# LayerNorm's mean from two float32r products, and nine operations of a depthwise convolution moved from VectorE to ScalarE and to transfers that add

## The chip, the cores and the metric

One core of a Trainium2 chip runs the whole layer. The metric is the device time of one execution in microseconds, the median of several runs. The five engines run their own instruction streams and meet through semaphores: TensorE (PE in the profile; its weight loads stand apart as PEld), VectorE (DVE), ScalarE (ACT), GpSimd (POOL) and SyncE (SP). SP issues the loads from HBM; POOL issues the transfers that add what they carry to what lies at their destination ("adding transfers" below).

## The reference, cut to what matters

A block of a streaming encoder over 512 positions and 1024 channels, in float32: a feed-forward half step, then a mixer that has a convolution branch and a gated linear attention branch beside each other, an output projection over both, a second feed-forward half step, and a gated input embedding. The change touches the convolution branch.

```python
h = h + 0.5 * _swiglu(_rmsnorm(h, ffn1_norm), ffn1_w_in, ffn1_w_out)
z = _rmsnorm(h, mix_norm) @ w_in
conv_a, conv_gt, q, k, v, r, g_lr = jnp.split(z, SPLIT_POINTS, axis=-1)
y_conv = _conv_module(conv_a, conv_gt, conv_w, conv_b, conv_ln_g, conv_ln_b)
y_gla = _gla(q, k, v, r, g_lr, gate_w_up, gate_b, gla_norm)
h = h + jnp.concatenate([y_conv, y_gla], axis=-1) @ w_out
...
def _conv_module(a, b, w_dw, b_dw, ln_g, ln_b):
    glu = a * jax.nn.sigmoid(b)                      # 512 channels
    y = causal depthwise convolution of glu, 31 taps per channel, + b_dw
    return jax.nn.silu(_layernorm(y, ln_g, ln_b))    # mean and variance over the 512 channels
```

## The kernel before, in words

Everything is held transposed, channels on the 128 partitions and the 512 positions along a row, so 512 channels are four blocks of 128x512. Products are exact to about float32: each operand is cut into a high part (a float32r copy, made by ScalarE, `high`) and a low part (what is left, made by a subtraction on VectorE, `low`, or by ScalarE and an adding transfer of POOL, `added`), and a product is the sum of high times high, high times low and low times high, each a float32r matmul.

The mixer is written out by hand in the order in which its work shall run. With `in_order(True)` each of TensorE, VectorE and ScalarE executes its own calls in the order of the code; POOL's and SP's calls are placed by the scheduler of the tile framework. The parts that matter here come in this order:

- The four blocks of `glu` are made one after the other (`glu_gate`, `glu_value`, `glu_out`). Each starts a generator, `conv_steps(c)`: one step that begins the accumulator `acc[c]` with the last tap and the bias (a TENSOR_SCALAR on VectorE), and 30 steps that each add one tap (a SCALAR_TENSOR_TENSOR on VectorE, in place on `acc[c]`). Nothing waits for them for long, so they are VectorE's filling: `taps(n)` runs n steps at some place of the code, in turn from the two oldest blocks that are not finished, so that neighbouring steps mostly belong to different accumulators. A call of `next` that finds a block finished counts as one of the n.
- q, k and v are projected; `tokblock(wv, t)` makes v for four blocks of 128 positions, t = 0 to 3. The attention scores follow (`scores`, where POOL clears the tiles `sc` first), then r (`tokblock(wr, t)`) with the attention outputs in between (`outputs`).
- The outputs' row norms: VectorE forms `ms`, POOL raises it to the power -1/2 (the row `rs<-ms,negh 128x16`), VectorE refines that to `rso`, ScalarE scales the outputs by it into four tiles `ytok`, VectorE multiplies each by `rt`, and TensorE transposes them (`ps<-ident,r` for the first, `ps<-ident,y` for the other three). At the same place POOL issues adding transfers for some weights that are wanted later (`px`, `sm`, `wa`; `early_parts`, `ohigh`).
- ScalarE and VectorE make the attention half of the mixer's result (`yg`, `gsplit`), and TensorE multiplies it with the output weights, block after block (`first_part(n, ...)`, twelve matmuls each).
- What is left of the convolution's taps runs then (`for steps in list(conv)`), the four accumulators are summed into `acc012`, and the mean over 512 channels is a product of a constant matrix of 1/512 with that sum, in the midst of `first_part(5, ...)`:

```python
mub = aux()
first_part(5, wo[5], {6: lambda: pe.matmul(mub, mean, acc012, start=True, stop=True)})
```

Both operands are float32 here. The variance, the normalisation and the second half of the output projection follow.

In the profile, tiles from one shared set of buffers (`bt`) carry the name of the pair they lie in: the sum `acc012` stands as `r`, the third block of `glu` as `glu` or `glu_3512`, the fourth as `en`; `cv` are the accumulators (3195 the third block's, 3196 the fourth's). All calls of an engine go through one recording line, L46, so rows are told apart by their tiles.

Of the kernel before, what the change touches and what calls it, by code (L numbers as in the profile page):

```python
# [8 lines left out]
F32 = mybir.dt.float32  # L9
F32R = mybir.dt.float32r  # L10
I32 = mybir.dt.int32
AF = mybir.ActivationFunctionType
ALU = mybir.AluOpType
PSUM = bass.MemoryType.PSUM

P = 128
SEQ = 512
# [3 lines left out]
D_CONV = 512  # L21
WIDTH = 31
PAD = WIDTH - 1
# [39 lines left out]
def block_kernel(ctx: ExitStack, tc: tile.TileContext, a: dict, out: bass.AP):  # L63
    nc = tc.nc
    pe, dve, act, pool = (Ordered(tc, e) for e in (nc.tensor, nc.vector, nc.scalar, nc.gpsimd))
# [6 lines left out]
    cp = ctx.enter_context(tc.tile_pool(name="const", bufs=1))  # L72
# [23 lines left out]
    def bt(dt=F32, s="a"):  # L96
        if dt not in other:
            t, other[dt] = bt2(dt, s)
            return t
        return other.pop(dt)  # L100
# [4 lines left out]
    def tmp(s, w=SEQ, dt=F32, bufs=2):  # L105
        return tp.tile([P, w], dt, tag=s, bufs=bufs, name=nm(s))
# [65 lines left out]
    cw = col[:, ncol - DC:]  # L172
# [5 lines left out]
    def vec(name, c, n=1):  # L178
        at = first_of[name] + c
        return col0[:, at:at + n] if at < DC else col[:, at - DC:at - DC + n]  # L180
# [8 lines left out]
    def split(src, s, alloc=bt):  # L189
        hi, lo = bt2(s=s) if alloc is bt else (alloc(F32R, s + "H"), alloc(F32R, s + "L"))  # L190
        h_, l_ = hi, lo
        if len(src.shape) == 3:
            h_, l_ = (t.rearrange("p (k c) -> p k c", k=src.shape[1]) for t in (hi, lo))
        act.copy(h_, src)
        dve.tensor_tensor(out=l_, in0=src, in1=h_.bitcast(F32), op=ALU.subtract)
        return hi, lo
# [26 lines left out]
    def high(r3):  # L223

        nk, nc_ = r3.shape[1], r3.shape[2]
        hi = wp.tile([P, 1024], F32R, tag="wh", bufs=6, name=nm("wh"))
        lo = wp.tile([P, 1024], F32R, tag="wl", bufs=6, name=nm("wl"))
        h3 = hi[:, :nk * nc_].rearrange("p (k c) -> p k c", k=nk)
        l3 = lo[:, :nk * nc_].rearrange("p (k c) -> p k c", k=nk)
        act.copy(h3, r3)  # L230
        return h3, l3, r3

    def low(w, engine=dve):
        h3, l3, r3 = w
        engine.tensor_tensor(out=l3, in0=r3, in1=h3.bitcast(F32), op=ALU.subtract)
        return h3, l3

    def added(w):

        h3, l3, r3 = w  # L240
        act.mul(l3, r3, -1.0)
        pool.dma_start(out=l3.bitcast(F32), in_=r3, accum_op=ALU.add)
        return w
# [29 lines left out]
    def zblock(w, x, mid={}):  # L273

        ps = bank()
        for k in range(DC):
            if k in mid:
                mid[k]()
            wh, wl = rows_of(w, k)
            mm3(ps, wh, wl, *x[k], k == 0, k == DC - 1)  # L280
        return ps
# [305 lines left out]
    made = []  # L587

    def constants():
        mean = cp.tile([P, P], F32, name="mean")  # L590
        pool.memset(mean, 1.0 / D_CONV)
        m1, m2 = (bt(s="m1")[:, 0:4 * CH].rearrange("p (c t) -> p c t", t=CH) for _ in range(2))
        mask = cp.tile([P, 4, CH], I32, name="mask")
        pool.memset(m1, 1.0)
        pool.memset(m2, 1.0)
        pool.affine_select(out=m1, in_=m1, compare_op=ALU.is_gt, fill=0.0, base=0,
                           pattern=[[0, 4], [-1, CH]], channel_multiplier=1)
        pool.affine_select(out=m2, in_=m2, compare_op=ALU.is_gt, fill=0.0, base=-CH,
                           pattern=[[0, 4], [-1, CH]], channel_multiplier=1)
        pool.tensor_copy(mask[0:CH], m1[0:CH])  # L600
        pool.tensor_copy(mask[CH:P], m2[CH:P])
        nbias = cp.tile([P, 2], F32, name="nbias")
        for j in range(2):
            dve.tensor_scalar(nbias[:, j:j + 1], vec("gate_b", j), -1.0, None, ALU.mult)
        made[:] = mean, mask, nbias
# [404 lines left out]

    glu, acc, conv = [], [cvt() for _ in range(4)], []

    def conv_steps(c):
        y, g, tap = acc[c], glu[c], cw[:, c * WIDTH:(c + 1) * WIDTH]
        dve.tensor_scalar(y, g, tap[:, PAD:WIDTH], vec("conv_b", c), ALU.mult, ALU.add)
        yield
        for w in range(PAD):
            late = PAD - w
            dve.scalar_tensor_tensor(out=y[:, late:], in0=g[:, 0:SEQ - late], scalar=tap[:, w:w + 1],
                                     in1=y[:, late:], op0=ALU.mult, op1=ALU.add)  # L1020
            yield
# [3 lines left out]
    def taps(n):  # L1025

        for _ in range(n):
            if not conv:
                return
            i = turn[0] % min(2, len(conv))  # L1030
            turn[0] += 1
            try:
                next(conv[i])
            except StopIteration:
                conv.pop(i)
# [8 lines left out]
    def glu_value(ps):  # L1044
        a1 = tmp("u1")
        dve.tensor_tensor(out=a1, in0=ps, in1=rsb, op=ALU.mult)
        return a1

    def glu_out(a1, sg):
        g = bt(s="glu")  # L1050
        dve.tensor_tensor(out=g, in0=a1, in1=sg, op=ALU.mult)
        glu.append(g)
        conv.append(conv_steps(len(glu) - 1))
# [77 lines left out]
    cums, epos, eneg, edec, decay, ends = [], [], [], [], [], []  # L1131
    taps(10)
    glu_out(glu_value(pa), sg)
    pb = zblock(w2b[1], hg)
    taps(5)
    for j in range(2):
# [92 lines left out]
    def scores(j, between):  # L1229
        p4s = [bank().rearrange("p (u c t) -> p u c t", u=2, t=CH) for _ in range(2)]  # L1230
        ss = []
        for i in range(2):
            s = bt(s="sc").rearrange("p (c t) -> p c t", t=P)
            pool.memset(s, 0.0)
            ss.append(s)
        for u, (kk, qq) in enumerate(((kneg[j], qdec[j]), (kpos[j], qneg[j]))):
            for c in range(0, NCH, 2):
                for i in range(2):
                    d = slice(i * HK, (i + 1) * HK)
                    for cc in (c, c + 1):  # L1240
                        s0 = (cc % 2) * CH
                        cs = slice(cc * CH, (cc + 1) * CH)
                        pe.matmul(p4s[i][s0:s0 + CH, u, c // 2, :], kk[d, cs], qq[d, cs], start=True, stop=True)
        hs = [slice(i * CH, (i + 1) * CH) for i in range(2)]
        for s, p4 in zip(ss, p4s):
            for h in hs:
                act.copy(s[h, :, h], p4[h, 0])
        between()
        for s, p4 in zip(ss, p4s):
            for h in hs:  # L1250
                dve.copy_predicated(s[h, :, h], mask[h], p4[h, 1])
        sc.extend(ss)
# [60 lines left out]
    for t in range(TB):  # L1313
        ps = tokblock(wv, t, {8: lambda: wr.append(high(raw_r[2])),
                             14: lambda: wr.append(high(raw_r[3]))} if t == 3 else {})
        if t == 0:
            wr += [added(high(raw_r[i])) for i in range(2)]
            k_out(1, k1)
            taps(3)
        elif t == 1:  # L1320
            taps(4)
        elif t == 2:
            taps(3)
        else:
            taps(5)
            low(wr[2])
            taps(2)
            low(wr[3])
        v = bt(s="v")
        act.activation(v, ps, AF.Copy, scale=rs2[:, t:t + 1])  # L1330
        vt.append(v)
        if t == 1:
            for j in range(2):
                scores(j, lambda: taps((6, 4)[j]))
            for j in range(2):
                kp = bank()
                for i in range(TB):
                    pe.transpose(kp[:, i * P:(i + 1) * P], kdec[j][:, i * P:(i + 1) * P], ident)
                kd = bt(s="kdt")
                act.copy(kd, kp)  # L1340
                kdt.append(kd)
# [40 lines left out]
    def first_part(n, w, mid={}):  # L1382
        ps = bank()
        part(ps, w, range(4, 8), True, False, mid)
        half[n] = (w, ps)
# [72 lines left out]
            pass  # L1458
    conv.clear()
    dve.tensor_tensor(out=acc012, in0=acc012, in1=acc[3], op=ALU.add)  # L1460
    low(wo[3])
    ffn2_in = a["ffn2_w_in"]
    wf = {i: Left(ffn2_in, 2 * i) for i in range(3)}
# [2 lines left out]
    w1.fetch("a11", "a12")  # L1466
    first_part(4, wo[4])
    mub = aux()
    first_part(5, wo[5], {6: lambda: pe.matmul(mub, mean, acc012, start=True, stop=True)})
    first_part(2, wo[2])  # L1470
    sqs, lln, yc = [], [], []
    for c in range(4):
# [339 lines left out]
        dve.scalar_tensor_tensor(out=q, in0=r, scalar=nh, in1=r, op0=ALU.mult, op1=ALU.mult)  # L1812
        dve.scalar_tensor_tensor(out=q, in0=q, scalar=1.5, in1=r, op0=ALU.add, op1=ALU.mult)

    def scaled_out(t, e, src, *queue):
        y = bt(s="y")
        act.activation(y, src, AF.Copy, scale=roots[t][2])
        put(t, e, y, *queue)

    def put(t, e, y, queue=nc.sync):  # L1820
        queue.dma_start(out=out[0, t * P:(t + 1) * P, e * SEQ:(e + 1) * SEQ], in_=y)

    def first_half(t, e):
        y = bt(s="y")
# [117 lines left out]
    first_half(0, 0)  # L1942
    scaled_out(0, 1, gained)
    newton(1)
    scaled_out(1, 0, hf[1], act)
    second_half(1, 1)


# [48 lines left out]
```

## Time and profile before

| | |
|---|---|
| median of 3 runs | 921.92 us (921.84 to 922.2) |
| the profiled execution | 921.48 us, of which the span from first to last instruction is 919.7 us |
| granted TensorE clock | 0.998 |
| busy: PE, PEld, DVE, ACT, POOL | 99%, 85%, 89%, 56%, 7% of the span |
| bytes moved by transfers | 118.89 MB, mean 129 GB/s |
| PE busy from 454 to 484 us | 15.90 of 15.90 us to 470, 4.92 of 5.00 us to 475, 8.70 of 9.00 us to 484 |
| DVE busy from 370 to 484 us | all of it but 2.5 us |

Rows of the timeline give the start in microseconds from the span's start, the time taken, the engine, the operation, output <- inputs, how many such instructions the row merges, and in brackets how long the engine sat idle before it and what released it. A matmul's time runs from its start to the end of its pipeline, so rows of PE overlap; what one costs is the distance from start to start. The convolution stands from 361 us (the first block's first step) to 483 us (the last sum).

### The profile page before, as it was taken

How to read it: one execution, taken by the hardware profiler on the slowest of the kernel's cores; microseconds unless marked ns; L12 is line 12 of the kernel's file. 1: busy time of each engine (PE TensorE's matmuls, PEld its weight loads, DVE VectorE, ACT ScalarE, POOL GpSimd, SP SyncE). 2: the span in 40 equal slices, each digit the busy share in tenths (PEclk: the TensorE clock that was granted, in tenths of full speed). 3: DMA queues.
4: the chain of work that ended last, by engine and by line, in shares of the span. 5: the costliest groups of instructions: out<-in, count | busy, mean ns of one | idle time of the engine just before them, and what ended most of it. 6: DMA issues, size and time to landing. Idle time of an engine off the chain costs nothing.

```text
span 919.7 us, 12838 instructions
## 1 busy us (share of the span) xinstructions
PE 910.7 (99%) x4948; PEld 779.7 (85%) x4948; DVE 816.7 (89%) x1090; ACT 511.7 (56%) x746; POOL 60.3 (7%) x76
## 2 busy tenths in 40 slices
PE   9999999999999999999999999999999999999996
PEld 8899888888888887788887889888888888888885
DVE  6699989999989766999996779899999999997896
ACT  7755354445454574463665875455445444556884
POOL 0120000000000111001130020000000000000121
PEclk9999999999999999999999999999999999999999
DMA  9534333224334692245572563333223322358454
GB/s 350 186 100 136 117 112 122 91 73 135 115 92 115 158 295 51 69 118 158 139 166 93 137 157 97 115 116 126 87 84 130 122 89 87 118 155 240 92 99 131
DMA packets 37149, 118.89 MB, mean 129 GB/s; under 512 B 4192, under 2 KB 4960, under 8 KB 37088
## 3 DMA queue, kind: packets, MB, share of 16 engines
q1 hardware_dynamic: 30176, 97.22, 31.8%
q0 software_dynamic: 6624, 20.58, 12.5%
q8 instruction: 39, 0.64, 0.3%
q10 hardware_dynamic: 288, 0.27, 0.1%
q14 instruction: 22, 0.18, 0.1%
HBM read 96.43 MB, written 2.10 MB: 107 GB/s over the span
## 4 chain that ended last, share of the span: by engine, by line
PE 96%; DVE 2%; ACT 1%; issue 0%; POOLq 0%
PE ps L46 56%; PE pd L46 40%; DVE cv L46 1%; ACT wa L46 0%; ACT sq L46 0%; DVE yg L46 0%; DVE r L46 0%; DVE y L46 0%; ACT r L46 0%; ACT sm L46 0%; ACT px L46 0%; POOLq L1993 0%; ACT s L46 0%; DVE u L46 0%; DVE g L46 0%
## 5 line engine op out<-in xcount | busy, mean ns | idle before, releaser
L46 DVE TENSOR_TENSOR wl<-wr,wh 128x1024 fp32r<-128x1024 f32 (+2 forms) x159 | 185.9, 1179 | 16.9 <-ACT wh L46 16.4
L46 ACT CAST wh<-wr 128x1024 fp32r<-128x1024 f32 (+2 forms) x177 | 175.4, 1023 | 14.4 <-PE ps L46 7.7
L46 PE MATMUL pd<-hg,wh 128*128 128x512 f32 x576 | 150.0, 391 | 0.0
L46 PE MATMUL ps<-act,wh 128*128 128x512 f32 x448 | 137.9, 389 | 0.0
L46 PEld LDWEIGHTS pd<-hg,wh 128*128 128x128 f32 x576 | 105.9, 188 | 21.1 <-DVE u L46 0.4
L46 PE MATMUL ps<-hg,wh 128*128 128x512 f32 (+1 forms) x448 | 117.0, 345 | 0.0
L46 PEld LDWEIGHTS ps<-act,wh 128*128 128x128 f32 x448 | 84.1, 188 | 17.5
L46 ACT ACTIVATE s<-g 128x512 f32<-128x512 f32 x48 | 30.4, 632 | 117.6 <-DVE g L46 117.6
L46 PE MATMUL pd<-t,wh 128*128 128x512 f32 x392 | 95.3, 391 | 0.0
L46 ACT COPY sq<-pd 128x1024 f32<-128x1024 f32 x45 | 45.8, 1017 | 86.7 <-PE pd L46 52.3
L46 PE MATMUL ps<-act,wl 128*128 128x512 f32 x224 | 87.1, 389 | 0.0
L46 PEld LDWEIGHTS ps<-hg,wh 128*128 128x128 f32 x448 | 78.0, 190 | 10.5 <-issue 0.5
L46 PEld LDWEIGHTS pd<-t,wh 128*128 128x128 f32 x392 | 71.4, 189 | 13.4
L46 PE MATMUL pd<-hg,wl 128*128 128x256 f32 (+1 forms) x544 | 81.5, 289 | 0.0
L46 PEld LDWEIGHTS pd<-hg,wl 128*128 128x128 f32 x544 | 73.9, 191 | 5.1
L46 PE MATMUL ps<-hg,wl 128*128 128x512 f32 (+1 forms) x224 | 77.0, 344 | 0.0
L46 ACT CAST wh<-sm 128x1024 fp32r<-128x1024 f32 x42 | 44.0, 1050 | 55.6 <-DVE sm L46 50.1
L46 DVE TENSOR_TENSOR wl<-sm,wh 128x1024 fp32r<-128x1024 f32 x42 | 51.0, 1219 | 5.1 <-ACT wh L46 5.1
L46 DVE TENSOR_TENSOR sq<-pd,sq 128x1024 f32<-128x1024 f32 x45 | 54.8, 1218 | 0.4 <-PE pd L46 0.4
L46 PE MATMUL ps<-wh,hg 128*128 128x512 f32 x176 | 54.4, 390 | 0.0
L46 PE MATMUL pd<-t,wl 128*128 128x256 f32 x392 | 52.4, 283 | 0.0
L46 PEld LDWEIGHTS pd<-t,wl 128*128 128x128 f32 x392 | 50.6, 191 | 1.5
(300 smaller groups left out, 1625.2 us busy)
## 6 DMA issues: line engine op xcount, KB each, us to landing
wr<-in_ffn_w_in SPq DMA_DIRECT2D x84, 512.0 KB, 3.6
wr<-in_ffn_w_out SPq DMA_DIRECT2D x32, 512.0 KB, 3.6
wl<-wr POOLq DMA_DIRECT2D x20, 512.0 KB, 5.4
wr<-in_ffn_w_out SPq DMA_DIRECT2D x16, 384.0 KB, 3.3
wr<-in_w_blocks SPq DMA_DIRECT2D x12, 512.0 KB, 5.7
wr<-in_w_rows SPq DMA_DIRECT2D x8, 512.0 KB, 3.8
wr<-in_w_out SPq DMA_DIRECT2D x8, 512.0 KB, 5.9
wq<-in_ple_w_gate SPq DMA_DIRECT2D x8, 512.0 KB, 4.3
```

What stands on the lines that cost most here:

```text
L46: inst = call(*args, **kwargs)
```

## The change

There are three edits.

1. The mean. `mean` becomes a float32r tile, and `acc012` is split into a high and a low part (`split`: a copy on ScalarE, a subtraction on VectorE). Two float32r products stand in place of the one float32 product, the first in front of block 5 of the twelve-matmul sequence, the second where the one stood.
2. The convolution. For the third block the first step and the taps 0 and 1, for the fourth the first step and the taps 0 to 4 are taken from VectorE. ScalarE begins the accumulator (`taps_begin`) and makes each of the seven taps as a tile of its own (`taps_apart`); adding transfers of POOL join these tiles and add them to the accumulator (`taps_add`): two for the third block, five for the fourth, some of 482 to 486 of 512 columns (about 247 KB each). VectorE's generator goes on from there.
3. The last output transfer but one is issued by SP and not by ACT.

```diff
 def constants():
-    mean = cp.tile([P, P], F32, name="mean")
-    pool.memset(mean, 1.0 / D_CONV)
+    mean = cp.tile([P, P], F32R, name="mean")
+    pool.memset(mean.bitcast(F32), 1.0 / D_CONV)
...
+def taps_apart(c, w, y):
+    late = PAD - w
+    act.activation(y[:, late:], glu[c][:, 0:SEQ - late], AF.Copy, scale=cw[:, c * WIDTH + w:c * WIDTH + w + 1])
+    return y
+
+def taps_begin(c):
+    act.activation(acc[c], glu[c], AF.Identity, bias=vec("conv_b", c), scale=cw[:, c * WIDTH + PAD:(c + 1) * WIDTH])
+
+def taps_add(y, x, w):
+    pool.dma_start(out=y[:, PAD - w:], in_=x[:, PAD - w:], accum_op=ALU.add)
+
+APART = (0, 0, 2, 5)
 def conv_steps(c):
     y, g, tap = acc[c], glu[c], cw[:, c * WIDTH:(c + 1) * WIDTH]
-    dve.tensor_scalar(y, g, tap[:, PAD:WIDTH], vec("conv_b", c), ALU.mult, ALU.add)
-    yield
-    for w in range(PAD):
+    if not APART[c]:
+        dve.tensor_scalar(y, g, tap[:, PAD:WIDTH], vec("conv_b", c), ALU.mult, ALU.add)
+        yield
+    for w in range(APART[c], PAD):
...
 glu_out(glu_value(pa), sg)               # the third block
+taps_begin(2)
+ta = [taps_apart(2, w, bt(s="ta")) for w in range(2)]
+taps_add(ta[1], ta[0], 0)
+taps_add(acc[2], ta[1], 1)
...
     if t == 0:                           # after tokblock(wv, 0)
-        wr += [added(high(raw_r[i])) for i in range(2)]
+        wr.append(added(high(raw_r[0])))
+        taps_begin(3)
+        ta = [taps_apart(3, w, tmp(("g1", "u1", "s")[w])) for w in range(3)]
+        taps_add(acc[3], ta[0], 0)
+        taps_add(ta[2], ta[1], 1)
+        wr.append(added(high(raw_r[1])))
+        ta += [taps_apart(3, w, tmp(("g1", "u1")[w - 3])) for w in (3, 4)]
+        taps_add(acc[3], ta[3], 3)
+        taps_add(ta[4], ta[2], 2)
         k_out(1, k1)
         taps(3)
...
     if t == 1:
         for j in range(2):
             scores(j, lambda: taps((6, 4)[j]))
+            if j == 0:
+                taps_add(acc[3], ta[4], 4)
...
 dve.tensor_tensor(out=acc012, in0=acc012, in1=acc[3], op=ALU.add)
+acch, accl = split(acc012, "sum")
...
-first_part(5, wo[5], {6: lambda: pe.matmul(mub, mean, acc012, start=True, stop=True)})
+first_part(5, wo[5], {5: lambda: pe.matmul(mub, mean, acch, start=True, stop=False),
+                      6: lambda: pe.matmul(mub, mean, accl, start=False, stop=True)})
...
-scaled_out(1, 0, hf[1], act)
+scaled_out(1, 0, hf[1])
```

Three places of the order of instructions are named by the prediction.

First, POOL's own queue while v is made (t = 0 and 1). `wl` are adding transfers for weights (512 KB each); before, three of them are followed by the clearing of the score tiles `sc`:

```order
L46 DMA wl_3591<-wr_3346 128x1024
L46 DMA wl_3805<-wr_3688 128x1024
L46 DMA wl_3810<-wr_3690 128x1024
L46 MEMSET sc_3855 128x512 x2
L46 MEMSET sc_3906 128x512 x2
L46 DMA wl_4047<-wr_4042 128x1024
```

and in the changed kernel, where `g`, `u` and `s` hold the fourth block's taps and `cv_3196` is its accumulator:

```order
L46 DMA wl_3811<-wr_3694 128x1024
L46 DMA cv_3196<-g_659_3816 128x482
L46 DMA s_3820<-u_660_3818 128x483
L46 DMA wl_3825<-wr_3696 128x1024
L46 DMA cv_3196<-g_664_3829 128x485
L46 DMA u_665_3831<-s_3820 128x484
L46 MEMSET sc_3876 128x512 x2
L46 MEMSET sc_3928 128x512 x2
L46 DMA cv_3196<-u_665_3831 128x486
L46 DMA wl_4069<-wr_4064 128x1024
```

Five transfers stand there now; each that reads or writes a tile of an earlier one waits until that one has landed, the last for the two in front of the clearings. VectorE's first step on `cv_3196` waits for the last.

Second, POOL's queue at the outputs' norm. Before, the power (TENSOR_TENSOR) stands in front of the transfer for `sm`:

```order
L46 DMA px_4041<-u_680_4038 128x256
L46 TENSOR_TENSOR rs_710_4256<-ms_4254,negh 128x16
L46 DMA sm_4234<-wr_4036 128x1024
L46 DMA wa_4277<-wr_4132 128x512
L46 DMA wa_4279<-wr_4132 128x512
```

and now behind it:

```order
L46 DMA px_4063<-u_686_4060 128x256
L46 DMA sm_4256<-wr_4058 128x1024
L46 TENSOR_TENSOR rs_716_4278<-ms_4276,negh 128x16
L46 DMA wa_4299<-wr_4154 128x512
L46 DMA wa_4301<-wr_4154 128x512
```

The transfer itself waits for ScalarE, which makes its source's partner.

Third, VectorE from the first multiplication of `ytok` by `rt` (the row on `st`) to the first `yg`. Before, the third block (`cv_3195`) and the fourth take turns:

```order
L46 TENSOR_TENSOR r_4271<-r_4271,st_4123 128x512
L46 SCALAR_TENSOR_TENSOR cv_3196<-en_3562,col,cv_3196 128x499
L46 SCALAR_TENSOR_TENSOR cv_3195<-glu_3512,col,cv_3195 128x510
L46 SCALAR_TENSOR_TENSOR cv_3196<-en_3562,col,cv_3196 128x500
L46 SCALAR_TENSOR_TENSOR cv_3195<-glu_3512,col,cv_3195 128x511
L46 SCALAR_TENSOR_TENSOR cv_3196<-en_3562,col,cv_3196 128x501
L46 TENSOR_TENSOR y_4297<-y_4297,r_4271 128x512
L46 TENSOR_TENSOR y_4297<-y_4297,y_4306 128x512
L46 TENSOR_TENSOR r_4372<-cv_3193,cv_3194 128x512
L46 TENSOR_TENSOR y_4306<-y_4306,r_4372 128x512
```

and now the third block is finished before this place:

```order
L46 TENSOR_TENSOR r_4293<-r_4293,st_4145 128x512
L46 SCALAR_TENSOR_TENSOR cv_3196<-en_3568,col,cv_3196 128x505
L46 SCALAR_TENSOR_TENSOR cv_3196<-en_3568,col,cv_3196 128x506
L46 SCALAR_TENSOR_TENSOR cv_3196<-en_3568,col,cv_3196 128x507
L46 SCALAR_TENSOR_TENSOR cv_3196<-en_3568,col,cv_3196 128x508
L46 SCALAR_TENSOR_TENSOR cv_3196<-en_3568,col,cv_3196 128x509
L46 TENSOR_TENSOR y_4319<-y_4319,r_4293 128x512
L46 TENSOR_TENSOR y_4319<-y_4319,y_4328 128x512
L46 TENSOR_TENSOR r_4393<-cv_3193,cv_3194 128x512
L46 SCALAR_TENSOR_TENSOR cv_3196<-en_3568,col,cv_3196 128x510
L46 TENSOR_TENSOR y_4328<-y_4328,r_4393 128x512
```

All five steps now follow each other on one accumulator, and one more step stands in front of the last multiplication (`y_4328`). Behind `yg`, where nine steps stood, none is left.

More of the change, by code (lines that the diff above doesn't have):

```diff
@@ L1813, in newton, with scaled_out, put @@
         dve.scalar_tensor_tensor(out=q, in0=q, scalar=1.5, in1=r, op0=ALU.add, op1=ALU.mult)
-    def scaled_out(t, e, src, *queue):
+    def scaled_out(t, e, src):
         y = bt(s="y")
         act.activation(y, src, AF.Copy, scale=roots[t][2])
-        put(t, e, y, *queue)
-    def put(t, e, y, queue=nc.sync):
-        queue.dma_start(out=out[0, t * P:(t + 1) * P, e * SEQ:(e + 1) * SEQ], in_=y)
+        put(t, e, y)
+    def put(t, e, y):
+        nc.sync.dma_start(out=out[0, t * P:(t + 1) * P, e * SEQ:(e + 1) * SEQ], in_=y)
     def first_half(t, e):
```

## The prediction

> **What bounds the kernel now.** I read the busy shares first, then the waits of TensorE's weight loads, then the chain that ended last, then the timeline around each edit.
>
> ```profile
> PE 910.7 (99%) x4948; PEld 779.7 (85%) x4948; DVE 816.7 (89%) x1090; ACT 511.7 (56%) x746; POOL 60.3 (7%) x76
> ```
>
> ```profile
> PEld ps L46 <- DVE r L46: 0.7, 1, 0.7
> PEld ps L46 <- DVE y L46: 0.7, 2, 0.5
> ```
>
> ```profile
> 124.74 5.44 PE ps L46 x24
> ```
>
> ```profile
> 420.00:423.00 3.00, 3.00 (x15) 2.48 (x14) 3.00 (x6) 0.69 (x1) 0.99 (x2) 1.00 1.01 167
> 429.00:434.00 5.00, 5.00 (x26) 4.23 (x25) 4.88 (x10) 2.84 (x7) 0.00 (x0) 1.00 0.00 0
> ```
>
> TensorE is the bound almost throughout: 99% busy, and in the chain 24 matmuls take 5.44 us, 0.227 us each, so its work is no shorter unless products go. The two rows of waits (total, count, longest) name the places where it waits for VectorE: once 0.7 us for `r`, the mean's operand, and twice, together 0.7 us, for `y`, the tiles `ytok` on their way to the transposes. VectorE at 89% is the bound only around there, from 454 to 484 us. The last two rows (stretch, its length, then the busy time of PE, PEld, DVE, ACT and POOL with their counts, the clock, the transfers' share and GB/s) are from the time in which v is made: PE and VectorE full, ScalarE (0.69 of 3 us) not, the transfers at a share of 1.01 and then, from 429 us, at none. Nine operations less on VectorE are therefore worth nothing by themselves; what counts is what PE waits for at 472 and 484 us.
>
> **The mean.**
>
> ```profile
> 483.03 0.39 PE L46 MATMUL ps<-yg,wa 128*128 128x512 f32 x1
> 483.72 1.12 PE L46 MATMUL ps<-r,mean 128*128 128x512 f32 x2 [0.30 <-DVE r L46]
> 484.28 1.95 PE L46 MATMUL ps<-yg,wa 128*128 128x512 f32 x6
> 486.07 0.40 PE L46 MATMUL ps<-yg,wh 128*128 128x512 f32 x1
> ```
>
> ```profile
> 475.94 6.99 DVE L46 SCALAR_TENSOR_TENSOR cv<-en,col,cv 128x503 f32<-128x503 f32 x9
> 482.97 0.69 DVE L46 TENSOR_TENSOR r<-r,cv 128x512 f32<-128x512 f32 x1
> ```
>
> The last product before the mean starts at 483.03 and costs one step, to 483.26. The mean starts at 483.72, so PE lost 0.46 us to the sum, which ends at 483.66. The six products behind it end their steps at 486.07; at 0.231 us each, the first took its turn at 484.68. Wait and float32 product cost 484.68 - 483.26 = 1.42 us. Two float32r products at 0.227 cost 0.45: -0.97 us. It needs the split sum in time: the nine taps from 475.94 are gone from there (seven not done by VectorE any more, two ahead of `yg`), so the sum can be ready about 2 us after the last `yg` (0.69 for the sum, 0.7 each for copy and subtraction), some 4 us before PE comes. That cover hides both parts of the split; a tap left over behind `yg` would use 0.78 of it.
>
> **The way to the transposes.**
>
> ```profile
> 472.19 0.66 PE L46 MATMUL ps<-ident,y 128*128 128x128 f32 x4
> ```
>
> ```profile
> 412.18 0.54 DVE L46 TENSOR_SCALAR cv<-glu,col 128x512 f32<-128x512 f32 x1
> 412.63 2.02 DVE L46 SCALAR_TENSOR_TENSOR cv<-glu,col,cv 128x502 f32<-128x502 f32 x3
> ...
> 433.30 0.54 DVE L46 TENSOR_SCALAR cv<-en,col 128x512 f32<-128x512 f32 x1
> ...
> 464.13 0.17 DVE L46 SCALAR_TENSOR_TENSOR rs<-rs,rs 128x16 f32<-128x16 f32 x1
> ...
> 471.45 0.68 DVE L46 TENSOR_TENSOR y<-y,r 128x512 f32<-128x512 f32 x1
> ```
>
> ```profile
> 464.48 1.24 ACT L46 ACTIVATE r<-ps,rs 128x128 f32<-128x128 f32 x4
> ```
>
> The last multiplication ends at 472.13 and the last transposes start at 472.19: PE has no slack against VectorE there. The order shows, between the first of these multiplications and the last (the row at 471.45), one tap more than before, and all five of its first taps on one accumulator. Alternating taps take 2.02 / 3, about 0.65 us; the nine chained ones 6.99 / 9 = 0.78. One tap more is +0.65, and four chained neighbours cost 4 x 0.13 = +0.52. From this goes ScalarE's slack: the root `rso` ends at 464.30, ScalarE's scaling starts at 464.48, so 0.17 of lateness at VectorE's side stays hidden. The last transposes come 1.0 us later. With the mean that makes +0.03: the two edits cancel, and what is left is the delay of `rso`, called d, which adds in full.
>
> **The delay d, through POOL.**
>
> ```profile
> 411.44 1.06 ACT L46 ACTIVATE wl<-wr 128x1024 fp32r<-128x1024 f32 x1
> ...
> 458.79 1.18 ACT L46 ACTIVATE sm<-wr 128x1024 fp32r<-128x1024 f32 x1
> ```
>
> ```profile
> 412.80 0.86 POOL L46 DMA_DIRECT2D wl<-wr  x1 [8.51 <-ACT wl L46]
> 417.86 0.86 POOL L46 DMA_DIRECT2D wl<-wr  x1 [4.20 <-ACT wl L46]
> 418.40 1.33 POOL L46 MEMSET sc<- 128x512 f32 x2
> ...
> 460.12 3.35 POOL L46 TENSOR_TENSOR rs<-ms,negh 128x16 f32<-128x16 f32 x1 [0.90 <-DVE ms L46]
> ```
>
> Before, the power starts at 460.12 when `ms` is there. Now the `sm` transfer stands ahead of it, and that waits for ScalarE until 458.79 + 1.18 = 459.97. An adding transfer starts 0.30 after its ScalarE row ends (412.50 to 412.80), so at 460.27. Its successor starts 0.54 later by the row at 417.86 (the clearing at 418.40) or 0.86 later by its length: power at 460.81 to 461.13, d = +0.69 to +1.01. I take 0.85, the middle; the row has one neighbour only. This is POOL's side of d; VectorE's side follows, and the later of the two counts.
>
> **The delay d, through VectorE.**
>
> ```profile
> 396.94 0.63 ACT L46 ACTIVATE s<-g 128x512 f32<-128x512 f32 x1 [6.01 <-DVE g L46]
> ...
> 415.56 1.05 ACT L46 CAST wh<-wr 128x1024 fp32r<-128x1024 f32 x1 [3.05 <-PE ps L46]
> ```
>
> ```profile
> wl<-wr POOLq DMA_DIRECT2D x1, 512.0 KB, 4.5
> wl<-wr POOLq DMA_DIRECT2D x1, 512.0 KB, 6.0
> wl<-wr POOLq DMA_DIRECT2D x1, 512.0 KB, 7.5
> px<-u POOLq DMA_DIRECT2D x1, 128.0 KB, 2.7
> ```
>
> `taps(n)` still runs n steps, so VectorE does as much before 454 us; only the kinds change. A first step costs 0.45 (412.18 to 412.63) and becomes a tap of 0.65: +0.2 at 412.18 and about +0.1 at 433.30, together 0.3. ScalarE's new work hides in its idle time: three operations of some 0.6 us (the form at 396.94) in the 6.01 us before 396.94, four in the 3.05 us before 415.56, two before `v` at 421.18.
>
> What is new is that the fourth block's first tap waits for POOL's fifth adding transfer, from about 433.5; I call that wait S. The transfers for the third block have from about 394 to 412 us. For the fourth, of about 247 KB, no row stands, so I bound them. The rows of issues (size, time from issue to landing) are those of 389.92 (alone), 412.80 and 417.86 (both while SP's loads run), and 458.36 (alone). From 128 KB in 2.7 us to 512 KB in 4.5 is 1.8 us for 384 KB: 247 KB alone take 2.7 + 1.8 x 119 / 384 = 3.3, and 1.2 where they follow another transfer without a gap; twice that, 2.4, where loads take half the engines' turns. The first `wl` lands at 412.80 + 6.0 = 418.8, the next two at 420 to 421.2 and 421.2 to 423.6, the second `wl` where it did, 417.86 + 7.5 = 425.4, or up to 428, the third and fourth at 426.6 to 430.4 and 427.8 to 432.8. The fifth waits for the fourth's landing and takes 0.3 to its issue and 3.3 more: 431.4 to 436.4, at the worst 437. S is 0 to 3.5; the share of 0.00 from 429 us on puts most of the chain nearer the short end, so I take 0 to 0.8. Then VectorE is late by 0.3 to 1.1 and POOL by 0.85; the larger counts, and d = 1.05 as a middle. The clearings of `sc`, now behind the fourth transfer's issue, move to 423 to 427, while ScalarE first writes there at 427.78: hidden, with the least to spare of all.
>
> **The output queue.**
>
> ```profile
> 915.98 0.38 ACTq L46 DMA_DIRECT2D out<-y  x1
> ```
>
> ```profile
> out<-y SPq DMA_DIRECT2D x6, 256.0 KB, 2.3
> out<-y ACTq DMA_DIRECT2D x1, 256.0 KB, 2.8
> ```
>
> ACT's issue at 915.98 lands last, at 918.78. Both on SP, the second is issued about 0.35 later and takes the 2.3 us of SP's rows: 916.35 + 2.3 = 918.65, or the 2.8 again, 919.15. Between -0.15 and +0.35; I take 0.
>
> **Sum.** -0.97 (mean) + 1.0 (way to the transposes) + 1.05 (d) + 0 (queue) = +1.1 us. The profiled execution took 921.48, 0.44 less than the median of 921.92; the change is added to the median: 923.0.
>
> **Rivals.**
>
> Rival one, slower: the five transfers form one chain and share with SP's loads. For it: the transfers' share of 1.01 at 420 to 423, and 6.0 and 7.5 us to landing where 4.5 was enough alone. Against it: from 429 to 434 us nothing else moves, so the last hops run alone. Price: if the fifth lands at 435.8, S = 2.3, d = 0.3 + 2.3 = 2.6, and the time is 924.5. It decides from a landing at 434.05, where VectorE (0.3 + 0.55) overtakes POOL (0.85); over 0.2% it is from S = 1.5 on, a landing at 435.0. The Trainium skill, "DMA: Bandwidth & Descriptors", section "Queues, rings and completion order", says that an engine goes round robin between the queues that have work, packet by packet; by that each hop beside loads about doubles, which is this rival. The trace agrees for one transfer (7.5 against 4.5 us); no run yet shows five. The Trainium skill's fit on the same page, section "Anatomy of one DMA — SWDGE (gpsimd) path", 2.0 us and the bytes at 436 GB/s, gives an estimate of 2.6 us for such a hop alone against the 3.3 that I take from rows; by it S is 0 more often than not.
>
> Rival two: it does what it says. POOL's lateness is hidden (the power's start is ruled by `ms`, as before), the taps do not stand in the way, and PE also loses part of the 0.7 us of waits for `y`: -0.97 - 0.2, some 920.8. Against it: the order puts `sm` ahead of the power, and 472.13 against 472.19 leaves nothing.
>
> Rival three: the terms cancel, 921.9. That is d near 0, with the tap rows paying as computed; it needs `sm`'s partner on ScalarE 0.8 us earlier than now, for which nothing speaks but ScalarE's idle share.
>
> **How the numbers follow.** Forecast (d 0.7 to 1.8, so 922.6 to 923.7): 0.45. Rival one (d 1.8 to 4, so 923.7 to 926): 0.35. Rival two: 0.10. Rival three: 0.10. About 0.2%, 1.84 us, is what a measurement of this kernel can tell from no change. The forecast and the two last rivals lie within it; rival two reaches beyond it only if the waits for `y` go in full and the tail gives too, 0.04 in all; of rival one nearly all lies beyond. So faster 0.04, same 0.63, slower 0.33. The range 921.3 to 925.9 leaves out rival two and the far end of rival one. The forecast's own is 922.6 to 923.7.
>
> **What the profile after would show.** The mean right: two float32r matmuls on `mean`, no wait of PE for `r`, and products in even steps around 484. The transposes: PE's wait for `y` grows from 0.7 to some 2.5 us in total, and five taps on one accumulator stand before it at 0.78. POOL's order: the power starts 0.7 to 1.0 later than `ms` allows, behind the `sm` issue. The fifth transfer: a wait of VectorE at its first tap on `en`, near 433.5, of 0 to 0.8 us; 1.5 or more is rival one. What would make all of it wrong is PE waiting somewhere in 412 to 450 us, at the scores or the states, because VectorE, held by S, comes late there too, or because the clearing of `sc` does.

## The result: 924.42 us against 921.88, and the profile after

| | before | after |
|---|---|---|
| median of 12 runs | 921.88 us (921.44 to 922.83) | 924.42 us (923.62 to 926.78) |
| ratio after to before | | 1.0029, 95% interval 1.002 to 1.0038 |
| profiled execution, its span | 921.48 us, 919.7 us | 924.39 us, 922.7 us |

The change makes the kernel 0.3% slower, and its runs scatter over 3.2 us where those before scattered over 1.4. The likeliest forecast was 923.0, with a range of 922.6 to 923.7 that the time misses; it lies in the range of rival one (924.5; 923.7 to 926), which had a chance of 0.35. One execution of the kernel called "the wait gone" below fell into a slower state and took 1853 us; it is left out of the scatter given for that kernel, and its median and ratio do not hang on it. The two profiled spans differ by 3.0 us, somewhat more than the medians (2.5), because the execution profiled before lay 0.4 us under its median.

The busy shares of after, and TensorE's waits for VectorE at the places in question (total, count, longest), the matmuls' own (PE) and those of the weight loads (PEld):

```profile
PE 910.3 (99%) x4948; PEld 779.5 (84%) x4948; DVE 811.7 (88%) x1082; ACT 518.0 (56%) x756; POOL 66.2 (7%) x83
```

```profile
PE ps L46 <- DVE y L46: 2.1, 2, 1.4
PE ps L46 <- DVE st L46: 1.6, 1, 1.6
PEld ps L46 <- DVE y L46: 3.0, 3, 1.6
```

VectorE has 5 us less work and TensorE the same, yet TensorE waits longer for VectorE: the wait for the sum of the mean is gone from both lists, the weight loads wait 3.0 us for `y` where it was 0.7, the matmuls themselves, which did not wait for `y` before, wait 2.1 us for it, and a wait for `st`, the states of the attention, is new. Where VectorE lost its time its timeline shows:

```profile
435.47 0.73 DVE L46 SCALAR_TENSOR_TENSOR cv<-en,col,cv 128x487 f32<-128x487 f32 x1 [1.94 <-DMA cv<-u]
...
446.94 0.29 DVE L46 COPY pq<-ps 128x128 f32<-128x128 f32 x1
...
462.36 0.17 DVE L46 TENSOR_SCALAR ms<-so 128x16 f32<-128x16 f32 x1
...
468.65 0.69 DVE L46 TENSOR_TENSOR r<-r,st 128x512 f32<-128x512 f32 x1 [0.56 <-ACT r L46]
469.26 3.88 DVE L46 SCALAR_TENSOR_TENSOR cv<-en,col,cv 128x505 f32<-128x505 f32 x5
...
475.52 0.69 DVE L46 TENSOR_TENSOR y<-y,r 128x512 f32<-128x512 f32 x1
```

The same places before:

```profile
444.52 0.29 DVE L46 COPY pq<-ps 128x128 f32<-128x128 f32 x1
...
459.86 0.17 DVE L46 TENSOR_SCALAR ms<-so 128x16 f32<-128x16 f32 x1
...
465.75 0.69 DVE L46 TENSOR_TENSOR r<-r,st 128x512 f32<-128x512 f32 x1
```

In the first row of after VectorE stands idle for 1.94 us at the first tap on the fourth accumulator, until the fifth adding transfer has landed. Everything that VectorE does afterwards is late: the first state copy starts at 446.94 (before: 444.52), `ms` at 462.36 (459.86), the first multiplication of `ytok` at 468.65 (465.75), the last at 475.52 (471.45; its row stands in the prediction). The lateness grows from 2.4 over 2.5 and 2.9 to 4.1 us, at the end by the one tap more and the five chained ones. VectorE has no spare time in which to catch up: before the change it was idle for 1.5 us in all from 370 to 484 us (the 2.5 in the table ahead of the prediction is too much).

The transfers themselves: POOL's issues, and for the second `wl` and the last three of the chain the time from issue to landing:

```profile
417.83 0.86 POOL L46 DMA_DIRECT2D wl<-wr  x1 [1.75 <-ACT wl L46]
420.94 0.86 POOL L46 DMA_DIRECT2D cv<-g  x1 [2.25 <-DMA cv<-g]
423.72 0.86 POOL L46 DMA_DIRECT2D u<-s  x1 [1.91 <-DVE cv L46]
424.25 2.26 POOL L46 MEMSET sc<- 128x512 f32 x4
432.15 0.86 POOL L46 DMA_DIRECT2D cv<-u  x1 [5.63 <-DMA u<-s]
```

```profile
wl<-wr POOLq DMA_DIRECT2D x1, 512.0 KB, 9.6
cv<-g POOLq DMA_DIRECT2D x1, 242.5 KB, 9.1
u<-s POOLq DMA_DIRECT2D x1, 242.0 KB, 7.9
cv<-u POOLq DMA_DIRECT2D x1, 243.0 KB, 3.3
```

The same 242 KB (the 247 of the text ahead of the prediction are thousands of bytes, the profile's KB are 1024) take 3.3 us alone and 7.9 to 9.1 us behind the 512 KB transfer and beside SP's loads. So the fourth lands at 423.72 + 7.9 = 431.6, the fifth is issued at 432.15 and lands at 435.45, when VectorE goes on. (The row of the fourth, `u<-s`, names a tap of VectorE as what ended its wait. The second, whose result it reads, landed at 415.22 + 7.8 = 423.0, 0.7 us before; in the other kernels with five transfers that distance is 0.5 to 0.75, so the landing is the likelier reason.) And the transfers that stood still from 429 us on before are now busy there (the last but one number is the transfers' share):

```profile
426.00:429.00 3.00, 3.00 (x135) 2.58 (x134) 3.00 (x6) 1.89 (x5) 0.51 (x2) 1.00 1.10 276
429.00:434.00 5.00, 5.00 (x26) 4.20 (x25) 4.45 (x9) 2.82 (x7) 0.86 (x1) 1.00 0.53 152
```

POOL at the outputs' norm, and TensorE at its three new or longer waits and at the mean:

```profile
462.40 0.86 POOL L46 DMA_DIRECT2D sm<-wr  x1 [1.33 <-ACT sm L46]
462.97 3.64 POOL L46 TENSOR_TENSOR rs<-ms,negh 128x16 f32<-128x16 f32 x1
```

```profile
450.41 3.59 PE L46 MATMUL ps<-v,sc 128*128 128x128 f32 x30 [1.58 <-DVE st L46]
...
473.80 1.26 PE L46 MATMUL ps<-ident,y 128*128 128x128 f32 x8 [1.37 <-DVE y L46]
...
476.26 0.65 PE L46 MATMUL ps<-ident,y 128*128 128x128 f32 x4 [0.74 <-DVE y L46]
...
486.66 0.40 PE L46 MATMUL ps<-sum,mean 128*128 128x512 f32 x1
486.89 0.85 PE L46 MATMUL ps<-yg,wa 128*128 128x512 f32 x3
487.58 0.40 PE L46 MATMUL ps<-sum,mean 128*128 128x512 f32 x1
```

`ms` is there at 462.36 + 0.17 = 462.53; the power starts at 462.97, 0.44 later, where it was 0.09 before. The two products of the mean take one step each (486.66 to 486.89, and 487.58 to 487.82, the start of the next).

### The profile page after: what moved, and what is told of

Same layout as the page of the kernel before. It is cut to its first block, busy times and chain, and to the rows that moved or that the text cites. A ratio compares the mean times of both kernels' runs of the same rounds, so it can differ in the third digit from the quotient of the medians.

```text
span 922.7 us, 12854 instructions
## 1 busy us (share of the span) xinstructions
PE 910.3 (99%) x4948; PEld 779.5 (84%) x4948; DVE 811.7 (88%) x1082; ACT 518.0 (56%) x756; POOL 66.2 (7%) x83
## 4 chain that ended last, share of the span: by engine, by line
PE 95%; DVE 2%; ACT 1%; issue 0%; DMA 0%; POOL 0%; POOLq 0%; SPq 0%
PE ps L46 55%; PE pd L46 40%; DVE cv L46 1%; ACT sq L46 0%; DMA wr<-in_first_w 0%; DVE y L46 0%; POOL rs L46 0%; DVE st L46 0%; ACT r L46 0%; DVE sc L46 0%; ACT wa L46 0%; DVE r L46 0%; ACT sm L46 0%; DVE wl L46 0%; DVE rs L46 0%
```

## The experiments

Three theories were set against each other. A: VectorE's wait for the fifth adding transfer is the loss, and it is handed on through the states and the outputs' norm to the transposes. B: the loss is POOL's order, `sm` ahead of the power. C: it is the taps between the multiplications of `ytok`. Each ratio below is against the kernel before on the same chip, with its 95% interval; the changed kernel stands at 1.0029.

**The mean alone** (kernel before, first edit only):

```diff
+acch, accl = split(acc012, "sum")
-first_part(5, wo[5], {6: lambda: pe.matmul(mub, mean, acc012, start=True, stop=True)})
+first_part(5, wo[5], {5: ... mean, acch ..., 6: ... mean, accl ...})
```

> The kernel before with the first edit alone (the mean by two float32r products), the convolution left on VectorE. My theory: the gain of 0.97 us at the mean hangs on the nine taps that the convolution edit takes away from behind yg. With them still there the sum ends at 483.66 as before, the high part on ScalarE at about 484.4, and PE, which now comes to the first product at about 482.6 (one block earlier), waits some 1.8 us: +0.9 us, 922.8, with a wait of PE for the tile sum of 1.5 to 2 us. Rival: the float32r products are worth their 0.97 us wherever they stand: 920.9 and no such wait.

Measured 922.8 us, ratio 1.0008 (0.9999 to 1.0017), +0.9 against the 921.93 beside it, and this row of TensorE:

```profile
484.63 0.50 PE L46 MATMUL ps<-sum,mean 128*128 128x512 f32 x1 [1.66 <-ACT sum L46]
```

The wait of 1.66 us is the one expected; the +0.9 itself lies at the edge of what the interval can tell from nothing. The float32r mean by itself gains nothing: a split needs its operand earlier by a copy and a subtraction, and the nine taps behind `yg` don't allow it.

**The convolution and the output queue without the mean** (changed kernel, mean as before):

> The changed kernel with the mean as before: one float32 product of the undivided sum, its place in the sequence as before. My theory: in the changed kernel no tap stands behind yg, so PE waits for nothing there, and the edit is worth only the product itself, about 0.96 us of float32 against 2 x 0.227: +0.5 us, 924.9, and no wait of PE for r. Together with the first edit alone (+0.9 us without the convolution edit) that says that each needs the other. Rival: the mean edit is worth its full 0.97 us here too, 925.4.

Measured 925.03 us, ratio 1.0033 (1.0021 to 1.0044). The difference to the changed kernel, 0.4 us by the ratios, is of the expected size, but the intervals overlap, so the runs alone don't settle it. That PE waits for no sum there the trace shows: the mean starts at 488.63, and until the six products behind it end their steps at 490.86 there are 2.23 us, of which six steps of 0.23 are theirs, so the float32 product costs 0.85 where two float32r ones cost 0.46. The profiled execution shows something else:

```profile
436.75 0.72 DVE L46 SCALAR_TENSOR_TENSOR cv<-en,col,cv 128x487 f32<-128x487 f32 x1 [2.45 <-DMA cv<-u]
```

The same wait was 1.94 in the changed kernel and 1.84 in the one with the power first (below): its length differs by up to 0.6 us between the three profiled executions, though none of the edits touches the transfers in front of it.

**The wait gone, the transfers unchanged.** VectorE's first tap on the fourth accumulator comes later, three more of the third block's first:

```diff
-    def taps(n):
+    def taps(n, k=2):
...
-            i = turn[0] % min(2, len(conv))
+            i = turn[0] % min(k, len(conv))
...
         elif t == 2:
-            taps(3)
+            taps(3, 1)
...
-                scores(j, lambda: taps((6, 4)[j]))
+                scores(j, lambda: taps((6, 4)[j], (2, 1)[j]))
```

> The changed kernel, with VectorE's first tap on the fourth accumulator moved some 4 us later (three more taps of the third block first, all transfers as they are). Theory A (VectorE's wait of 1.94 us for the fifth adding transfer at 433.5 is what makes the kernel slow): that wait is gone, PE's wait of 1.6 us for the states at 449 us is gone, d falls from 2.9 to 0.7-1.0, and the time is 922.3 to 922.9. Theory B (POOL's order, sm ahead of the power, is the cause): 924 to 924.4, the power still starts 2.5 us or more later than before. Theory C (the taps between the multiplications of ytok are the cause): 924 to 924.4, unchanged.

Measured 923.43 us, ratio 1.0016 (1.0007 to 1.0025): 1.0 us back by the medians (1.2 by the ratios), not the 1.5 to 2.1 that A expected, and not unchanged, as B and C expected. Both waits are gone, VectorE's at the transfer and TensorE's for the states. At least part of what is missing went into pace: in this order the third block ends earlier and more taps follow each other on one accumulator, as behind `ms`:

```profile
462.03 2.29 DVE L46 SCALAR_TENSOR_TENSOR cv<-en,col,cv 128x500 f32<-128x500 f32 x3
```

That is 0.76 each where alternating ones take 0.65. Counted from POOL's first `wl` near 413 us, the first multiplication of `ytok` comes 0.5 us later here (467.72 - 413.34) than in the next kernel (466.86 - 412.98), which has no wait either and is 0.7 us faster.

**The chain of transfers earlier.** The 512 KB transfer for the second r weight goes behind the first four; the call of the fifth moves a little down in the code, but keeps its place in POOL's order, behind the clearings:

```diff
             taps_add(ta[2], ta[1], 1)
-            wr.append(added(high(raw_r[1])))
             ta += [taps_apart(3, w, tmp(("g1", "u1")[w - 3])) for w in (3, 4)]
             taps_add(acc[3], ta[3], 3)
             taps_add(ta[4], ta[2], 2)
+            wr.append(added(high(raw_r[1])))
...
-                scores(j, lambda: taps((6, 4)[j]))
-                if j == 0:
-                    taps_add(acc[3], ta[4], 4)
+                scores(j, lambda: (taps_add(acc[3], ta[4], 4) if j else None, taps((6, 4)[j])))
```

> The changed kernel, with the 512 KB transfer for the second r weight issued behind the fourth block's first four adding transfers instead of between the second and the third. Theory A: the third and fourth land some 3 us earlier, the fifth is issued at about 429 and lands at about 432.5 to 433.5, VectorE waits 0 to 0.3 us instead of 1.94, and the time is 922.3 to 923.0. Theories B and C: 924 to 924.4. A third outcome, that the loads of SP hold the third and fourth back whatever stands before them, would leave the wait above 1 us and the time above 923.4.

Measured 922.71 us, ratio 1.001 (1.0001 to 1.0019). The third and the fourth transfer, and VectorE's first tap on the fourth accumulator:

```profile
cv<-g POOLq DMA_DIRECT2D x1, 242.5 KB, 6.0
u<-s POOLq DMA_DIRECT2D x1, 242.0 KB, 5.2
```

```profile
433.68 0.72 DVE L46 SCALAR_TENSOR_TENSOR cv<-en,col,cv 128x487 f32<-128x487 f32 x1
```

Without the 512 KB ahead of them in their queue they take 6.0 and 5.2 us instead of 9.1 and 7.9, VectorE's row carries no wait, and 1.7 us of the 2.5 are back. This is theory A's outcome, with every one of the transfers still made; B and C foresaw no change. The loads still cost something (5.2 to 6.0 against 3.3 alone; in the three later kernels with this order 4.7 to 7.4), so the third outcome named there holds in part, without deciding.

**Three taps instead of five** on ScalarE for the fourth block (`APART = (0, 0, 2, 3)`, three transfers there):

> The changed kernel with taps 0 to 2 of the fourth block on ScalarE instead of 0 to 4: three adding transfers there instead of five, the third (a sum of two taps) issued at about 424 behind the 512 KB transfer. Theory A: the last lands at 429 to 432, before VectorE asks at 433.5, no wait there and none of PE at the states; VectorE has two taps more, both behind yg, where nothing waits for them: 922.4 to 923.0, as with the five and the r transfer behind them. Rival: what counts is how much VectorE is relieved: then it is as slow as the changed kernel or slower (924.4 or more).

Measured 922.85 us, ratio 1.0008 (0.9999 to 1.0017). The third transfer takes 9.7 us here, but it is the last, and VectorE, which has two taps more, does not wait. Less relief and a faster kernel: the amount by which VectorE is relieved does not decide. Together with the kernel of the earlier chain, which kept all five transfers, this says that what counts is whether the last one lands in time.

**The third block alone** (`APART = (0, 0, 2, 0)`, none of the fourth's transfers):

> The changed kernel without the fourth block's part: its first step and taps 0 to 4 stay on VectorE, only the third block's two adding transfers are made. Theory A: no wait at the fourth accumulator, POOL keeps the order power, sm; d is 0 to 0.4; the taps between the multiplications of ytok are the same five in a row and one as in the changed kernel, so +1.2 us stays at the transposes; the mean gives -0.97. Together 922.1 to 922.6. If the adding transfers as such were dear, the third block's two would show: VectorE's first tap there would wait at 412.

Measured 922.1 us beside 922.17, ratio 0.9997 (0.9988 to 1.0006): no change that can be told, at the low end of the expectation. VectorE does not wait at its first tap on the third accumulator. Two transfers that nobody needs for a good ten microseconds after they land cost nothing that shows.

**The power first.** ScalarE makes the partner of `sm` behind its activation of `r`, and POOL issues the power before the transfer:

```diff
-        early_wh[:] = added((wh, wl, early_w))[:2]
+        early_wh[:] = [wh, wl]
...
         if t == 1:
+            added((*early_wh, early_w))
             oload(2)
```

> The changed kernel, with the partner of sm made on ScalarE behind the activation of r, so that POOL issues the power ahead of the sm transfer as before the change. Theory A: only the 0.35 us go that the power waits for the sm issue now (ms ready at 462.53, power at 462.97): 923.9 to 924.2; the 1.94 us wait of VectorE and the 1.6 us of PE for the states stay. Theory B: the time falls to 922.0 to 922.6. Theory C: unchanged, 924.4.

Measured 923.97 us, ratio 1.0024 (1.0014 to 1.0033). The difference of 0.4 us to the changed kernel is the size that A gave, though the intervals overlap; B's 2 us are excluded.

**No taps between the multiplications.** On top of the earlier chain, `taps((0, 2, 5, 1)[t])` becomes `taps((0, 0, 0, 0)[t])`, so that seven taps run behind `yg`; then the power first as well; then two of the seven put into waits of VectorE for ScalarE:

> The kernel with the r transfer behind the fourth block's adding transfers (922.71), and in addition none of the fourth block's taps between the multiplications of ytok: seven run behind yg. Theory: the six taps there (3.87 us in a row and 0.74) are what is left of the loss, now that the fifth transfer is no longer waited for. PE's waits for y (1.9 us) fall to below 0.5, the seven taps and the split sum are done when PE comes to the mean (about 482.3 us), within 0.5 us: 920.5 to 921.2. Rival: what is left comes from POOL's order (power 0.4 us behind ms): then 922.3.

> As the one before, and POOL's power ahead of the sm transfer. With no tap between the multiplications of ytok, ScalarE's scaling ends about 1 us before PE asks for the transposes, so the 0.5 us that the power comes earlier lie off the path: the same time as the one before, 920.5 to 921.2, within 0.2 us. If it is faster by 0.4 or more, the root is still on the path.

> The last kernel (no taps between the multiplications of ytok, power ahead of sm), with two of the seven taps behind yg put where VectorE waits for ScalarE anyway: one ahead of the first multiplication (a wait of 1.36 us there), one ahead of the third (1.96 us). Theory: both lie in waits, five taps are left behind yg, the split sum comes 1.5 us earlier and the wait of PE for it (0.5 us at the weight load, some 0.25 at the matmuls) goes: 0.1 to 0.4 us faster than the last kernel. Rival: a tap delays the root's users in spite of the wait, PE waits for y again, and it is as slow or slower.

Measured 921.35 us, ratio 0.9992 (0.9983 to 1.0); with the power first 920.57, ratio 0.9984 (0.9975 to 0.9993); filled 920.36, ratio 0.9984 (0.9975 to 0.9993). The rival of the first (922.3) is out, but 921.35 is 0.15 above what was expected, and the second expectation failed: with the power first the time is 0.8 us less by the medians, though the intervals overlap, and 0.5 us by the traces (from the issue of `px` to the mean's first product 484.00 - 459.44 = 24.56 us without it, 482.69 - 458.62 = 24.07 with it). ScalarE's scaling ends later than I reckoned, so the root is still on the path. With the power first:

```profile
466.42 0.69 DVE L46 TENSOR_TENSOR r<-r,st 128x512 f32<-128x512 f32 x1 [1.36 <-ACT r L46]
467.46 0.69 DVE L46 TENSOR_TENSOR y<-y,r 128x512 f32<-128x512 f32 x1 [0.34 <-ACT y L46]
470.11 0.69 DVE L46 TENSOR_TENSOR y<-y,y 128x512 f32<-128x512 f32 x1 [1.96 <-ACT y L46]
```

The third multiplication waits for ScalarE until 470.11 and ends at 470.80, and the last follows to 472.01; TensorE starts the last transposes at 472.06. TensorE's weight load for the mean waited there, too:

```profile
PEld ps L46 <- ACT sum L46: 0.5, 1, 0.5
```

With two taps put into VectorE's waits this row is gone and the time is 0.2 us less, which is as expected and less than the runs can tell from nothing. Both last kernels are faster than before, by about 1.5 us, and than the changed one by about 4.

Taken one behind the other, the order of the transfers (924.42 to 922.71), the taps between the multiplications (to 921.35) and the power (to 920.57) are worth 1.7, 1.4 and 0.8 us. A is the largest part of the loss and not all of it; what C names was in the forecast as +1.0.

## Why the prediction was right and wrong, step by step

- **The mean: right.** -0.97 forecast; 1.42 - 2 x 0.23 = 0.96 measured, with no wait. The runs add that this holds only together with the convolution edit: the 0.46 of waiting for the sum go by that edit alone, the product is worth some 0.4, and without that edit the split makes TensorE wait 1.66.
- **The way to the transposes: right.** From the first multiplication to the last it took 471.45 - 465.75 = 5.70 us and takes 475.52 - 468.65 = 6.87: +1.17, the 0.65 + 0.52 of the sum, without the 0.17 that ScalarE's slack was to take. The five chained taps run at 3.88 / 5 = 0.78. The last kernels, which have none of them there, get that back.
- **S, the wait for the fifth transfer: mis-sized.** The bounds held (0 to 3.5), and the landings of the third, the fourth and the fifth lie in theirs, but I took 0 to 0.8 and it is 1.94. The failing sentence is that the share of 0.00 from 429 us on puts most of the chain nearer the short end. That share was read in the trace of a kernel without the new transfers. With them the second `wl` takes 9.6 us where it took 7.5, the share from 429 to 434 is now 0.53, and the third and fourth transfer land at 430.0 and 431.6, in the upper part of my bounds (426.6 to 430.4, 427.8 to 432.8). From a landing to the issue that waits for it 0.5 to 0.7 us pass, not the 0.3 taken. By the Trainium skill, "DMA: Bandwidth & Descriptors", section "Queues, rings and completion order", an engine goes round robin between the queues that have work, as quoted for rival one; the traces agree in direction, with 5.2 to 6.0 us beside loads against 3.3 alone. Of the 5.8 us by which 9.1 exceeds 3.3, though, 3.1 are the 512 KB ahead in the same queue, as the run with that transfer moved shows. The fit in the Trainium skill, the same page, section "Anatomy of one DMA — SWDGE (gpsimd) path", gave an estimate of 2.6 us for a hop alone; measured is 3.3, as interpolated from the rows.
- **d, the larger of two delays: wrong in form.** I let POOL's order hide behind VectorE's lateness. TensorE, which came 1.6 us late out of the states, made ScalarE's squares and with them the partner of `sm` late as well; so the power, with `ms` late by 2.5, still waits for the `sm` issue, 0.35 us longer than before. The delays add, 2.50 and 0.35 to the 2.85 us by which the power starts later. The same order cost 0.35 and not the 0.7 to 1.0 forecast. VectorE's own part, beside S, is 2.42 - 1.94 at the first state copy, 0.5 where the sum had 0.3.
- **The states: not in the sum.** That TensorE would wait there stood only among the things that would make it all wrong. It is the same lateness met earlier: the 1.58 us that TensorE loses at 450.41 it does not lose again at 473.80, where it comes later itself. With the fifth transfer in time the wait is gone.
- **The output queue: right.** From the last scaling to the end of the span 919.7 - 915.23 = 4.47 before, 922.7 - 918.34 = 4.36 after: -0.1, forecast 0.
- **The sum.** -0.96 + 1.17 + 2.9 (`ytok`'s first multiplication, 465.75 to 468.65) - 0.1 = +3.0, the difference of the spans.
- **Rival one: right in its mechanism, in part lucky in its number.** It had a wait of 2.3 us and hid POOL's order behind it. The wait is 1.94; with that, its own sum gives 0.3 + 1.94 for d and 924.2 us. What it did not have, POOL's 0.35, 0.2 more of VectorE's own and ScalarE's lost slack of 0.17, raises that, and the medians, which differ by 2.5 where the spans differ by 3.0, lower it again, to the 924.42 that stand beside its 924.5.

## What to carry to other kernels

Work taken from a busy engine and given to a chain of transfers is paid for at the first instruction that needs its end: reckon when the last link lands with the new transfers themselves in the queue, not in the gaps that the old trace shows, and put large transfers that nobody wants yet behind the chain. Where an engine has no idle time, a wait of two microseconds reaches every later user in full, as here, and delays on two engines add when the second engine is late because of the first. Filling work belongs behind the last urgent result, alternating between accumulators where it can; put into waits it cost nothing here and gained nothing that the runs can tell.

## What was not expected of the hardware

An adding transfer of 242 KB took 3.3 us alone. The third and the fourth of the fourth block's chain took 4.7 to 7.4 us beside loads, in the four kernels that issue the 512 KB behind them, and 7.9 to 9.7 with those 512 KB ahead of them in their queue. The kernels that wait for such a landing also scattered more: the three with the wait ranged over 2.0 to 3.2 us (the changed one from 923.62 to 926.78), all the others over 0.8 to 1.5 (922.27 to 923.73 for the same transfers in an order that lands in time). The waits of 1.84, 1.94 and 2.45 us in the three executions profiled fit to this; that they make the scatter is not shown.
